# The second half of the delta heads: one exponential per head in a block behind the last query Silu, the norm factor by a GpSimd power

## The chip, the cores and the metric

The kernel runs on one core of a Trainium2 chip. The metric is the time of one execution on the device in microseconds. The kernel before has three timed runs, and one execution taken by the profiler.

## The reference, cut to what matters

One block of a network: modulated norm, projections, a dilated attention (8 heads) and a gated delta rule (8 heads) side by side, an output projection, and a feed-forward part. The change concerns the delta heads, 64 wide, over 1024 tokens.

```python
qkv = jax.nn.silu(_causal_conv(jnp.concatenate([q, k, v], axis=-1), conv_w))
...
q = _l2norm(q.reshape(shp)) * HEAD_DIM ** -0.5
k = _l2norm(k.reshape(shp))          # x * rsqrt(sum(x*x) + EPS)
...
gcum = jnp.cumsum(g...)              # per chunk
diff = gcum[..., :, None] - gcum[..., None, :]
decay = jnp.where(causal, jnp.exp(jnp.where(causal, diff, 0.0)), 0.0)
a_mat = jnp.where(strict, jnp.einsum('nbhcd,nbhed->nbhce', k_beta, kc) * decay, 0.0)
...
qk = jnp.where(causal, jnp.einsum('nbhcd,nbhed->nbhce', qc, kc) * decay, 0.0)
```

In the kernel a chunk has 128 tokens, so there are 8 chunks. For each head a tile of 128 keys x (8 chunks x 128 queries) holds `exp(G_query - G_key)` times the factor `rk` that normalises the key, and zero above the diagonal. Both score products are multiplied with it as they leave the accumulators.

## The kernel before

**Two halves of heads.** `delta(0)` handles heads 0 to 3, `delta(1)` heads 4 to 7. A half consists of: convolution and Silu of its keys and queries (`conv`, L550), their transposes and square sums (`delta_turn`, L729), the decay tiles and the score products (`delta_prep`, L754), the values (`delta_v`, L845), the inverse (`delta_inverse`, L867) and the scan over the chunks (`delta_scan`, L973). The convolutions, transposes and square sums of the second half's four tensors (cv0 and cv1 keys, cv2 and cv3 queries) are done in `delta_early` (L1195), which is called at the end of `delta(0)`. A finished one is stored to DRAM (L1202), and `delta(1)` loads it back (L1221).

**Fill.** TensorE (PE) does other projections between the steps of the delta part. `others()` (L1148) yields them in fixed order: z0, then kd, qd and vd of the second half, z1, then va, and key and query projections of the attention. Each of the first five is 20.48 us by its own count (8 tiles of 2.56 for z). `turn(name)` (L576) takes as much of it as the table `FILL` says for that step, and puts the step behind the last fill instruction on PE; `hold` (L1181) does the same ahead of an inverse, by `LEVELS`: 4 us behind qd for the first half, 46 us behind z1 for the second. The steps of the first half's inverse have 0.64 each, lc0_0 1.92; sb0_6 has 1.92, trq3_0False 2.56, kk1_0_0_q 6.4, kk1_0_0_k 0.64, trv2_0 12.8, trv3_0 10.24.

**What drains a z tile.** A tile of z is 24 matmuls (L613) into one of two accumulator banks with the tag "g"; `z_evac` (L630) drains it by a Silu on ScalarE (ACT, L634), GpSimd (POOL) multiplies it by the norm's gain (L635), and SyncE's queue (SP) stores it. All projections use these two "g" banks in turn.

**Order.** Each engine works through its instructions in the order in which the planner has put them; what is traced earlier has precedence, `urgent()` raises it, and `tc.issue_after(ins)` puts what is traced in its block behind `ins` on that engine. Buffers with one tag are used in turn: "dt" (two buffers) serves, one after the other, the first half's nt, tt and tn of the inverse, then cv0 to cv3, and then eb2 and eb3. "lu" (five) serves the decay tiles `dt0_*` and `dt1_*`, the values vd and the inverse U. "s" and "t" are two accumulator banks each.

**The decay tiles before.** `delta_rows` (L704) loads, for each head, the row of G broadcast to all partitions, and POOL cuts it at the diagonal with -1e30 (L716). `delta_prep` forms `lr = -0.5 * ln(rk + eps) - Gc` (L765, L766, L768) from the square sums `rk`, and `rk = exp(-0.5 * ln)` (L767). Then ACT does 32 exponentials of 128x128 for each half, one for every head and chunk, with `lr` as its bias (L771). Near its end `delta_prep` loads `eb` (rows of G for 64 partitions each, L832), takes its exponential (L839) and multiplies q by it on POOL (L840).

ACT holds one table of functions at a time; the profile shows a load (ACT_TABLE_LOAD) wherever Silu, Ln and Exp follow each other.

Of the kernel before, what the change touches and what calls it, by code (L numbers as in the profile page):

```python
# [10 lines left out]
F32 = mybir.dt.float32  # L11
F32R = mybir.dt.float32r
AF = mybir.ActivationFunctionType
# [5 lines left out]
P = 128  # L19
# [17 lines left out]
EPS = 1e-6  # L37
# [45 lines left out]
def build(tc, I, out):  # L83
# [35 lines left out]
    )  # L119
    eps1 = const([P, 1], "eps1")  # L120
    nc.vector.memset(eps1, EPS)
    mhalf = const([P, 4], "mhalf")
    nc.vector.memset(mhalf, -0.5)

    const([P, 88], "end")

    def small(name, shape, src):
        t = const(shape, name)
# [418 lines left out]
        wt = [scratch(f"wt{i}_", NF, [P, HALF]) for i in range(4)]  # L547


    def conv(ci, xp, dst):  # L550
        nc.scalar.activation(dst, xp, AF.Copy, scale=cw[:, ci, 3:4])
        for s_ in range(1, 4):
            nc.vector.scalar_tensor_tensor(
                out=dst[:, s_:T], in0=xp[:, 0 : T - s_], scalar=cw[:, ci, 3 - s_ : 4 - s_], in1=dst[:, s_:T],
                op0=ALU.mult, op1=ALU.add,
            )
        nc.scalar.activation(dst, dst, AF.Silu)

    kd, qd = {}, {}
    last, taken = [None], [None]  # L560
# [69 lines left out]
    def z_evac(g):  # L630
        def f(tb, ps):
            zt = pv.tile([P, 256], F32, name=f"zt{g}_{tb}", tag="ev", bufs=4)
            with urgent():
                taken[0] = nc.scalar.activation(zt, ps[:, 0:256], AF.Silu)  # L634
# [69 lines left out]
    def delta_rows(g):  # L704

        dts = []
        for hl_ in range(4):
            dt_ = pd.tile([P, 8, P], F32, name=f"dt{g}_{hl_}", tag="lu", bufs=5)
            nc.sync.dma_start(
                dt_,  # L710
                bass.AP(
                    tensor=_.G.tensor, offset=_.G[0:1, :].offset + (32 * g + hl_) * P,
                    ap=[[0, P], [4 * P, 8], [1, P]],
                ),
            )
            sel[g] = nc.gpsimd.affine_select(  # L716
                out=dt_, in_=dt_, pattern=[[0, 8], [1, P]], compare_op=ALU.is_ge, fill=-BIG,
                base=0, channel_multiplier=-1,
            )
            dts.append(dt_)  # L720
        return dts

    def delta_norms(g):
        n = {}
# [4 lines left out]
    def delta_turn(g, kind, q, src, norms=None, keep=False):  # L729

        hp = 2 * g + q
        if keep:
            ktt = pd.tile([P, 8, P], F32, name=f"kt{hp}", tag="kt", bufs=2)
        for hf in range(2):
            ps = sbank(f"tr{kind}{hp}_{hf}{norms is None}")
            with turn(f"tr{kind}{hp}_{hf}{norms is None}"):
              for j in range(4):
                nc.tensor.transpose(
                    ps[:, j * P : (j + 1) * P], src[:, (4 * hf + j) * P : (4 * hf + j + 1) * P], ident
                )  # L740
# [12 lines left out]

    def delta_prep(g, st, norms, kt, lts):  # L754

        rk, eq, nbp, nbg, kds, lr = (norms[k] for k in ("rk", "eq", "nbp", "nbg", "kds", "lr"))
        gs = slice(32 * g, 32 * g + 32)
# [1 line left out]
        def g3(t):  # L759
            return t[:, gs].rearrange("p (n h) -> p n h", n=8)  # L760

        eqf = eq.rearrange("p n h -> p (n h)")

        if g == 1:
            nc.scalar.activation(lr, rk, AF.Ln, bias=eps1)  # L765
        nc.vector.tensor_scalar(out=lr, in0=lr, scalar1=-0.5, scalar2=None, op0=ALU.mult)  # L766
        nc.scalar.activation(rk, lr, AF.Exp)  # L767
        nc.vector.tensor_tensor(out=lr, in0=lr, in1=g3(Gc), op=ALU.subtract)  # L768
        for h in range(4):
            for n in range(8):  # L770
                nc.scalar.activation(lts[h][:, n], lts[h][:, n], AF.Exp, bias=lr[:, n, h : h + 1])  # L771
# [50 lines left out]
        for q in range(2):  # L822
            hp = 2 * g + q
            with tc.issue_after(sel[g].ins):
                nc.gpsimd.tensor_tensor(
                    out=kt[q].rearrange("p n (e d) -> p n e d", e=2),
                    in0=kt[q].rearrange("p n (e d) -> p n e d", e=2),
                    in1=bc(kds[:, :, 2 * q : 2 * q + 2], 64), op=ALU.mult,
                )
            eb = pr.tile([P, 8, P], F32, name=f"eb{hp}", tag="dt", bufs=2)  # L830
            for e in range(2):
                nc.sync.dma_start(  # L832
                    eb[64 * e : 64 * e + 64],
                    bass.AP(
                        tensor=_.G.tensor, offset=_.G[0:1, :].offset + (32 * g + 2 * q + e) * P,
                        ap=[[0, 64], [4 * P, 8], [1, P]],
                    ),
                )
            nc.scalar.activation(eb, eb, AF.Exp)  # L839
# [350 lines left out]
    def fetch(i, name):  # L1190
        xp = pr.tile([P, T], F32, name=f"xp_{name}", tag="xp", bufs=2)
        nc.sync.dma_start(xp, _.pj[i])
        return xp

    def delta_early():  # L1195

        for j in range(4):
            kind, q = ("k", j) if j < 2 else ("q", j - 2)
            t = pr.tile([P, T], F32, name=f"cv{j}", tag="dt", bufs=2)
            conv((4 if kind == "k" else 0) + 2 + q, fetch(j, f"{kind}{2 + q}"), t)  # L1200
            delta_turn(1, kind, q, t, norms=norms[1])
            nc.sync.dma_start(_.cv[j], t)  # L1202

    marks = {}
    norms = [delta_norms(g) for g in range(2)]

    def delta(g):
        st = {}
        kt = []
        for j in range(4):  # L1210
# [9 lines left out]
            else:  # L1220
                nc.sync.dma_start(t, _.cv[j])  # L1221
                if kind == "k":
                    kt.append(delta_turn(g, kind, q, t, keep=True))
        delta_prep(g, st, norms[g], kt[0:2], delta_rows(g))
        if g == 1:
            until(lambda: "vd" in done)
        delta_v(g, st, [lambda q=q: vxp[q] if g == 0 else fetch(4 + q, f"v{2 + q}") for q in range(2)])
        delta_inverse(g, st)
        until(lambda: ("qd", "z1")[g] in done)
        delta_scan(g, st)  # L1230
        if g == 0:
            delta_early()

    delta(0)
    delta(1)
    until(lambda: EARLY - 1 in done)
    run(mods)

# [763 lines left out]
```

## Time and profile before

| | us |
|---|---|
| three runs | 1399.05, 1403.87, 1405.15 (median 1403.87) |
| the profiled execution | 1399.13 |
| its span | 1397.3 |
| mean granted clock of PE | 0.991 |
| PE busy | 1343.9 |
| VectorE (DVE) busy | 878.8 |
| ACT busy | 661.4 |
| POOL busy | 283.6 |

The span goes from the first instruction to the last on the engines. A row of a timeline gives the start, the duration, the engine, the line, and the tiles "out<-in"; brackets at its end show how long the engine sat idle before it, and what released it. A row of a group gives busy time and mean, then idle time and its releasers. PE's rows overlap by the depth of its pipeline, so the pitch between starts says more of its rate than a duration does. Matmul tiles carry names such as `g_z` (projection), `kk_q` and `kk_k` (score products), `trk`, `trq` and `trv` (transposes of keys, queries and values).

### The profile page before, as it was taken

The page shows a single profiled execution, that of the slowest core. Times are in us where ns is not written, and L with a number is a line of the kernel's source. Part 1 is how long each engine was busy: PE and PEld are TensorE (multiplying, and loading weights), DVE is VectorE, ACT ScalarE, POOL GpSimd, SP SyncE. Part 2 cuts the span into 40 slices and gives each one's busy share as a digit, 9 for nine tenths or more (in the row PEclk, how much of TensorE's full clock was granted, in tenths as well). Part 3 has the DMA queues.
Part 4 walks back from the last instruction along what each step waited for, and adds up shares of the span by engine and source line. Part 5 has one row for each costly group of instructions (what it writes and reads, how often), then busy time and mean ns, then how long its engine had stood idle before and what let it go on. Part 6 is the DMA issues. An engine that isn't in the chain of part 4 may idle for free.

```text
span 1397.3 us, 24428 instructions
## 1 busy us (share of the span) xinstructions
PE 1343.9 (96%) x8984; PEld 1109.9 (79%) x8984; DVE 878.8 (63%) x1677; ACT 661.4 (47%) x1287; POOL 283.6 (20%) x267
## 2 busy tenths in 40 slices
PE   8999999998999899999999999999999999999998
PEld 5778877888888777778877788888888888888876
DVE  3688484656836433676238977667575776474497
ACT  4498424356234254775157633333333333444455
POOL 2346412443213244443262000000000000000000
PEclk9999999999999999999999999999999999999999
DMA  8666575486352455541584355455453665766585
GB/s 310 230 190 168 160 212 168 131 259 184 106 152 69 124 141 177 152 110 58 187 269 151 113 159 181 158 163 173 133 200 108 213 210 191 255 222 192 195 262 197
DMA packets 169872, 245.68 MB, mean 176 GB/s; under 512 B 32566, under 2 KB 73831, under 8 KB 169752
## 3 DMA queue, kind: packets, MB, share of 16 engines
q1 hardware_dynamic: 169752, 244.12, 55.3%
q8 instruction: 71, 1.16, 0.3%
q14 instruction: 49, 0.40, 0.1%
HBM read 181.30 MB, written 67.48 MB: 178 GB/s over the span
## 4 chain that ended last, share of the span: by engine, by line
PE 53%; DVE 5%; DMA 3%; issue 2%; ACT 2%; POOL 1%; SPq 0%; DVEq 0%; ACTq 0%; POOLq 0%
PE wua L1596 9%; PE wga L1596 8%; PE X L1796 6%; PE wuc L1596 4%; PE wgc L1596 4%; PE wo L590 4%; PE g_a L590 3%; PE wgb L1596 2%; PE Z L1796 2%; PE Y L1796 2%; PE wub L1596 2%; PE y L1353 2%; PE tr L1332 2%; PE S L1308 1%; PE S L1309 1%
## 5 line engine op out<-in xcount | busy, mean ns | idle before, releaser
L1586 DVE TENSOR_TENSOR wl_db<-wr_db,wh_db 128x512 fp32r<-128x512 f32 x77 | 52.9, 690 | 66.4 <-ACT wh_db L1585 66.4
L1585 ACT CAST wh_db<-wr_db 128x512 fp32r<-128x512 f32 x77 | 47.4, 620 | 85.7 <-PE X L1796 39.4
L1312 DVE CUSTOM_DVE_ANT_0 X<-S,ng 128x512 f32<-128x512 f32 (+3 forms) x64 | 36.9, 587 | 57.2 <-PE S L1309 43.7
L1319 POOL TENSOR_SCALAR X<-X,sc 128x128 f32<-128x128 f32 (+7 forms) x64 | 48.7, 764 | 76.3 <-DVE sc L1318 72.3
L1796 PE MATMUL X<-wl_db,wh_da 128*128 128x512 f32 x160 | 62.4, 390 | 0.3 <-DVE wl_db L1586 0.3
L1796 PE MATMUL X<-wh_db,wl_da 128*128 128x512 f32 x160 | 62.3, 389 | 0.0
L1796 PE MATMUL X<-wh_db,wh_da 128*128 128x512 f32 x160 | 62.3, 389 | 0.0
L1317 ACT ACTIVATE X<-X,sc 128x128 f32<-128x128 f32 (+7 forms) x64 | 49.5, 775 | 24.3 <-DVE sc L1312 22.7
L1586 DVE TENSOR_TENSOR wl_da<-wr_da,wh_da 128x512 fp32r<-128x512 f32 x77 | 52.8, 685 | 3.7 <-ACT wh_da L1585 3.6
L1585 ACT CAST wh_da<-wr_da 128x512 fp32r<-128x512 f32 x77 | 47.5, 616 | 15.0 <-DMA wr_da<-ao_d 8.1
L590 PE MATMUL g_a<-hh,wh_a 128*128 128x512 f32 x128 | 52.7, 412 | 0.0
L590 PE MATMUL wo<-yl,wh_wo 128*128 128x512 f32 x128 | 50.6, 396 | 1.9 <-DVE yl L1416 1.9
L590 PE MATMUL g_a<-hh,wl_a 128*128 128x512 f32 x128 | 51.7, 404 | 0.0
L590 PE MATMUL wo<-yh,wh_wo 128*128 128x512 f32 x128 | 51.6, 406 | 0.0
L590 PE MATMUL g_a<-hl,wh_a 128*128 128x512 f32 x128 | 51.4, 401 | 0.0
L590 PE MATMUL wo<-yh,wl_wo 128*128 128x512 f32 x128 | 51.1, 399 | 0.0
L1332 PE MATMUL tr<-ident,X 128*128 128x128 f32 x288 | 45.8, 278 | 5.1 <-POOL X L1319 2.4
L1585 ACT CAST wh_wg_s<-wg_s 128x512 fp32r<-128x512 f32 x33 | 20.5, 623 | 57.6 <-PE wuc L1596 24.4
L1332 PEld LDWEIGHTS tr<-ident,X 128*128 128x128 f32 x288 | 32.8, 140 | 17.0 <-POOL X L1319 6.2
L231 POOL TENSOR_TENSOR wl_wo<-wr_wo,wh_wo 128x512 fp32r<-128x512 f32 x24 | 32.2, 1344 | 59.1 <-ACT wh_wo L230 54.9
L1585 ACT CAST wh_wu_s<-wu_s 128x512 fp32r<-128x512 f32 x33 | 20.4, 621 | 43.8 <-PE wga L1596 17.2
L1585 ACT CAST wh_wg<-wr_wg 128x512 fp32r<-128x512 f32 x31 | 19.2, 622 | 46.3 <-PE wua L1596 18.9
(553 smaller groups left out, 4370.0 us busy)
## 6 DMA issues: line engine op xcount, KB each, us to landing
wm<-in_wada SPq DMA_DIRECT2D x44, 512.0 KB, 6.3
wr_da<-ao_d SPq DMA_DIRECT2D x77, 256.0 KB, 3.1
wr_wu<-in_wu SPq DMA_DIRECT2D x50, 256.0 KB, 2.7
wr_wg<-in_wg SPq DMA_DIRECT2D x48, 256.0 KB, 2.9
ao_d<-a SPq DMA_DIRECT2D x44, 256.0 KB, 2.4
wr_wd<-in_wdn SPq DMA_DIRECT2D x44, 256.0 KB, 3.0
wr_db<-wt_d SPq DMA_DIRECT2D x44, 256.0 KB, 2.7
ao_d<-as SPq DMA_DIRECT2D x33, 256.0 KB, 2.0
```

The lines of the kernel that those rows point to most:

```text
L231: (eng or nc.gpsimd).tensor_tensor(out=lo[:, :n], in0=raw[:, :n], in1=hi[:, :n].bitcast(F32), op=ALU.subtract)
L590: last[0] = nc.tensor.matmul(ps, a[:, w0], b[k0 + k4][:, cs], start=(i == 0), stop=(i == n - 1))
L1308: nc.tensor.matmul(ps[:, 0 : c1 - c0], QS[:, qs], KS[:, c0:c1], start=True, stop=False)
L1312: nc.vector.tensor_tensor_reduce(out=X[:, c0:c1], in0=ps[:, 0 : c1 - c0], in1=ng[:, u + c0 : u + c1], scale=1.0, scalar=(3e38 if m is None ...
L1317: nc.scalar.activation(X[:, 0:nk], X[:, 0:nk], AF.Exp, scale=-1.0, bias=m, accum_out=sc[:, 2:3])
L1319: nc.gpsimd.tensor_scalar(out=X[:, 0:nk], in0=X[:, 0:nk], scalar1=sc[:, 3:4], scalar2=0.0, op0=ALU.mult, op1=ALU.add)
L1332: nc.tensor.transpose(ps[:, (kb - c0) * P : (kb - c0 + 1) * P], X[:, kb * P : kb * P + P], ident)
L1353: ins = nc.tensor.matmul(yps[64 * e : 64 * e + 64, (q % 4) * P : (q % 4 + 1) * P], va[:, kb, 64 * e : 64 * e + 64], ets[q % 2][e][:, kb, : ...
L1585: nc.scalar.copy(hi, src)
L1586: (eng or nc.vector).tensor_tensor(out=lo, in0=src, in1=hi.bitcast(F32), op=ALU.subtract)
L1596: nc.tensor.matmul(ps, a[:, w0], b, start=(first and k == 0 and n_ == 0), stop=(k == 3 and n_ == 2), skip_group_check=True,)
L1796: nc.tensor.matmul(bank[b], a[:, ts_], w, start=(first and n_ == 0), stop=(last and n_ == 2), skip_group_check=True,)
```

## The change

The first half is computed as before. For the second half:

- `delta_early` stores cv ahead of its transposes, and behind the Silu of the last query (cv3) it calls the new `delta_exps`: the four decay rows are loaded and cut, DVE subtracts Gc from each, ACT takes one exponential of 128x1024 for each head, and then those of eb2 and eb3; the six stand in this order behind the Silu.
- Every Silu that is traced after that, those of `conv` and of `z_evac`, is put behind the last of the six (`behind`).
- `rk` is formed by POOL at the end of each key's turn: `(rk + EPS) ** -0.5`, on 16 elements of each partition. `delta_prep` has no Ln and no Exp of the norm in this half; DVE multiplies each decay tile by `rk` instead, 128x1024 each.
- `mhalf` grows from 4 to 16 columns, and a pad of the constants shrinks by 12.

```diff
-    mhalf = const([P, 4], "mhalf")
+    mhalf = const([P, 16], "mhalf")
...
-    const([P, 88], "end")
+    const([P, 76], "end")
...
+    behind = [None]
+
     def conv(ci, xp, dst):
...
-        nc.scalar.activation(dst, dst, AF.Silu)
+        with tc.issue_after(behind[0].ins) if behind[0] else ExitStack():
+            return nc.scalar.activation(dst, dst, AF.Silu)
...
     def z_evac(g):
...
-            with urgent():
+            with urgent(), tc.issue_after(behind[0].ins) if behind[0] else ExitStack():
                 taken[0] = nc.scalar.activation(zt, ps[:, 0:256], AF.Silu)
...
(delta_rows)
+            if g:
+                nc.vector.tensor_tensor(
+                    out=dt_, in0=dt_, op=ALU.subtract,
+                    in1=bc(Gc[:, 32 * g : 32 * g + 32].rearrange("p (n h) -> p n h", n=8)[:, :, hl_], P),
+                )
             dts.append(dt_)
         return dts
+
+    def delta_exps(last):
+
+        lts = delta_rows(1)
+        ebs = [delta_eb(1, q) for q in range(2)]
+        for t in (*lts, *ebs):
+            with tc.issue_after(last.ins):
+                last = nc.scalar.activation(t, t, AF.Exp)
+        behind[0] = last
+        return lts, ebs
+
+    def delta_eb(g, q):
+
+        eb = pr.tile([P, 8, P], F32, name=f"eb{2 * g + q}", tag="dt", bufs=2)
+        for e in range(2):
+            nc.sync.dma_start(
+                eb[64 * e : 64 * e + 64],
+                bass.AP(
+                    tensor=_.G.tensor, offset=_.G[0:1, :].offset + (32 * g + 2 * q + e) * P,
+                    ap=[[0, 64], [4 * P, 8], [1, P]],
+                ),
+            )
+        return eb
...
(delta_turn)
+        if norms and kind == "k" and g:
+            v = norms["rk"][:, :, 2 * q : 2 * q + 2]
+            nc.gpsimd.tensor_scalar(out=v, in0=v, scalar1=EPS, scalar2=None, op0=ALU.add)
+            nc.gpsimd.tensor_tensor(
+                out=v, in0=v, in1=mhalf.rearrange("p (n e) -> p n e", e=2), op=ALU.pow,
+            )
...
-    def delta_prep(g, st, norms, kt, lts):
+    def delta_prep(g, st, norms, kt, lts, ebs):
...
-        if g == 1:
-            nc.scalar.activation(lr, rk, AF.Ln, bias=eps1)
-        nc.vector.tensor_scalar(out=lr, in0=lr, scalar1=-0.5, scalar2=None, op0=ALU.mult)
-        nc.scalar.activation(rk, lr, AF.Exp)
-        nc.vector.tensor_tensor(out=lr, in0=lr, in1=g3(Gc), op=ALU.subtract)
-        for h in range(4):
-            for n in range(8):
-                nc.scalar.activation(lts[h][:, n], lts[h][:, n], AF.Exp, bias=lr[:, n, h : h + 1])
+        if g == 0:
+            nc.vector.tensor_scalar(out=lr, in0=lr, scalar1=-0.5, scalar2=None, op0=ALU.mult)
+            nc.scalar.activation(rk, lr, AF.Exp)
+            nc.vector.tensor_tensor(out=lr, in0=lr, in1=g3(Gc), op=ALU.subtract)
+            for h in range(4):
+                for n in range(8):
+                    nc.scalar.activation(lts[h][:, n], lts[h][:, n], AF.Exp, bias=lr[:, n, h : h + 1])
+        else:
+            for h in range(4):
+                nc.vector.tensor_tensor(out=lts[h], in0=lts[h], in1=bc(rk[:, :, h], P), op=ALU.mult)
...
-            eb = pr.tile([P, 8, P], F32, name=f"eb{hp}", tag="dt", bufs=2)
...
-            nc.scalar.activation(eb, eb, AF.Exp)
+            if ebs:
+                eb = ebs[q]
+            else:
+                eb = delta_eb(g, q)
+                nc.scalar.activation(eb, eb, AF.Exp)
...
(delta_early, for each of the four)
-            conv((4 if kind == "k" else 0) + 2 + q, fetch(j, f"{kind}{2 + q}"), t)
+            last = conv((4 if kind == "k" else 0) + 2 + q, fetch(j, f"{kind}{2 + q}"), t)
+            nc.sync.dma_start(_.cv[j], t)
+            if j == 3:
+                made = delta_exps(last)
             delta_turn(1, kind, q, t, norms=norms[1])
-            nc.sync.dma_start(_.cv[j], t)
+        return made
...
-        delta_prep(g, st, norms[g], kt[0:2], delta_rows(g))
+        delta_prep(g, st, norms[g], kt[0:2], *(made or (delta_rows(g), None)))
...
-        if g == 0:
-            delta_early()
+        return None if g else delta_early()
...
-    delta(0)
-    delta(1)
+    delta(1, delta(0))
```

More of the change, by code (lines that the diff above doesn't have):

```diff
@@ L829, in delta_prep @@
                 )
-            eb = pr.tile([P, 8, P], F32, name=f"eb{hp}", tag="dt", bufs=2)
[L831 to L839, printed above, removed]
+            if ebs:
[3 more added lines that the diff above has]
+                nc.scalar.activation(eb, eb, AF.Exp)
             nc.gpsimd.tensor_tensor(
@@ L1199, in delta_early, with delta @@
             t = pr.tile([P, T], F32, name=f"cv{j}", tag="dt", bufs=2)
-            conv((4 if kind == "k" else 0) + 2 + q, fetch(j, f"{kind}{2 + q}"), t)
+            last = conv((4 if kind == "k" else 0) + 2 + q, fetch(j, f"{kind}{2 + q}"), t)
+            nc.sync.dma_start(_.cv[j], t)
+            if j == 3:
+                made = delta_exps(last)
             delta_turn(1, kind, q, t, norms=norms[1])
-            nc.sync.dma_start(_.cv[j], t)
+        return made
     marks = {}
     norms = [delta_norms(g) for g in range(2)]
-    def delta(g):
+    def delta(g, made=None):
         st = {}
```

## The prediction

> **What bounds the kernel now.** I read the page's engine shares first, then the busy time by stretch around the change, then who waits for whom on PE there, then the timelines.
>
> ```profile
> PE 1343.9 (96%) x8984; PEld 1109.9 (79%) x8984; DVE 878.8 (63%) x1677; ACT 661.4 (47%) x1287; POOL 283.6 (20%) x267
> 305.00:315.00 10.00, 9.14 (x98) 8.19 (x96) 4.50 (x13) 9.81 (x16) 4.07 (x5) 1.00 0.92 320
> 315.00:325.00 10.00, 10.00 (x91) 8.91 (x90) 4.76 (x9) 9.48 (x27) 6.82 (x5) 1.00 0.75 245
> 335.00:345.00 10.00, 6.24 (x63) 5.70 (x63) 5.63 (x8) 3.56 (x4) 0.64 (x2) 0.77 0.62 167
> 345.00:355.00 10.00, 10.00 (x100) 9.67 (x99) 6.24 (x6) 1.91 (x4) 0.95 (x1) 0.89 0.34 98
> ```
>
> PE is busy 96% of the span, so over the whole kernel an idle microsecond of PE is a microsecond of time, unless something later waits anyway. In the stretches the columns are length, then busy time of PE, PEld, DVE, ACT and POOL, then the clock. From 305 to 325 us ACT is full too (9.81 and 9.48 of 10). But PE keeps running beside it (9.14 and 10.00); it loses time only behind it, at 335:345 (6.24), where the clock falls to 0.77 and is still 0.89 in the next stretch.
>
> ```profile
> PE trv L857 <- ACT vd L557: 3.8, 1, 3.8
> PE yt L1065 <- DVE o L1055: 1.2, 1, 1.2
> PE trq_0False L738 <- ACT cv L557: 0.9, 1, 0.9
> PE kk_q L800 <- DMA qd<-cv_d: 0.9, 1, 0.9
> PE kk_k L800 <- DVE qk L806: 0.3, 1, 0.3
> ```
>
> Those are all of PE's waits from 285 to 345 us: 7.1 us in sum. Only the first is long: the first value transpose of the second half (trv2, L857) waits for a Silu that ACT gives late. Everything else of ACT's load is covered by projections that fill PE (z1 at L613, then va). That cover is the point on which the change turns:
>
> ```profile
> 260.99 0.37 PE L613 MATMUL g_z<-wh_z,hh 128*128 128x256 f32 x1
> ...
> 278.59 0.38 ACT L634 ACTIVATE zt<-g_z 128x256 f32<-128x256 f32 x1 [0.33 <-PE g_z L613]
> 286.98 0.38 ACT L634 ACTIVATE zt<-g_z 128x256 f32<-128x256 f32 x1 [1.35 <-PE g_z L613]
> 289.86 0.38 ACT L634 ACTIVATE zt<-g_z 128x256 f32<-128x256 f32 x1 [2.50 <-DMA zl<-zg_d]
> ...
> 313.88 0.37 ACT L634 ACTIVATE zt<-g_z 128x256 f32<-128x256 f32 x1
> ```
>
> The rows of ACT are drains of the z1 projection: eight tiles of 24 matmuls in two "g" banks. The first tile starts at 260.99, tile 0 is drained at 278.59, tile 1 at 286.98, tile 2 at 289.86, tile 7 at 313.88.
>
> **The change, part by part.**
>
> *ACT gets lighter.*
>
> ```profile
> L771 ACT ACTIVATE dt<-dt,lr 128x128 f32<-128x128 f32 x32 | 9.7, 397 | 0.0
> L765 ACT ACTIVATE lr<-rk,eps 128x32 f32<-128x32 f32 x1 | 0.3, 321 | 0.0
> L767 ACT ACTIVATE rk<-lr 128x32 f32<-128x32 f32 x1 | 0.2, 229 | 0.0
> 303.12 1.28 ACT L765 ACT_TABLE_LOAD   x1
> L839 ACT ACTIVATE eb<-eb x4: 1039/1045/1058, 143.2 to 330.0; 128x1024 f32<-128x1024 f32 x4
> ```
>
> Removed for the second half: 32 small exponentials (9.7 us), Ln and Exp of the norm (0.3 and 0.2). Added: 4 of 128x1024 as L839's, 1.05 each, 4.2. The two of eb move. Six table loads in this part (before L765, twice back to Silu, L767, L771, and L557 of vd) become two, 4 x 1.28 = 5.1 saved. ACT loses 9.7 + 0.5 + 5.1 - 4.2 = 11.1 us. On the path only what PE waited for counts: the 3.76 us at trv2 and the 0.27 at kk_k can go, 4.0 in sum.
>
> *DVE and POOL get heavier.*
>
> ```profile
> L875 DVE TENSOR_TENSOR nt<-nt,bpr x2: 1216/1221/1226, 172.1 to 353.2; 128x1024 f32<-128x1024 f32 x2
> L1053 POOL TENSOR_TENSOR of<-of,mhalf x16: 1006/1007/1122, 252.6 to 472.3; 128x4 f32<-128x4 f32 x16
> 302.53 2.59 DVE L553 SCALAR_TENSOR_TENSOR cv<-xp_q,cw,cv 128x1022 f32<-128x1022 f32 x2
> ```
>
> Four subtractions of Gc and four multiplications by rk, each 128x1024 with a broadcast operand as L875: 8 x 1.22 = 9.8 us of DVE. The subtractions stand around the two query convolutions, whose last step (L553) ends at 302.53 + 2.59 = 305.1. One row tile is loaded long before, so three can get in the way: between 0 and 3 x 1.22 = 3.7 us later; I take 0, because the convolution is traced ahead of them. The multiplications hide behind z1 matmuls that PE still has to do (below); without that cover they would cost 4.9. On POOL two adds and two powers on 16 elements for Ln and Exp: a power of 4 elements takes 1.01, so 16 lie between 1.01 and 4 x 1.01; POOL is busy 4.07 of 10 us at 305:315, and rk is first used after that. Zero. The larger mhalf is paid for by the smaller pad: no address moves.
>
> *What is moved, and the wait it makes.* The block (4 row loads, 4 selects on POOL, 4 subtractions, 4 + 2 exponentials, 4 half loads of eb) goes from the second half's preparation to behind the Silu of cv3. And every Silu traced later must stand behind the block on ACT. The fill that the program takes ahead of its steps can be added up: until qd is done 62.1 us, 4.5 by LEVELS, 11.5 at the sixteen steps of the four inverses, 1.9 at sb0_6, together 80.0 when the block is traced; z1 begins at 4 x 20.48 = 81.92. So all eight drains of z1 come behind it, those that ran at 278.59 and 286.98 too. Queued behind them: tile 2 of z1 needs tile 0's bank, and the rest of z1, va and kk1_0_0 (which waits for 6.4 us of fill, into tile 2) come after it. PE runs out when tile 1 is done, at about 286.9, and stays so until the block ends.
>
> When does it end? Its last link is the exponential of eb3. That tile takes the buffer of cv3 ("dt", two buffers), so it waits until cv3 is transposed and its store has landed.
>
> ```profile
> 306.54 1.06 ACT L557 ACTIVATE cv<-cv 128x1024 f32<-128x1024 f32 x1
> ...
> cv_d<-cv SPq DMA_DIRECT2D x3, 512.0 KB, 6.3
> eb<-G_d SPq DMA_DIRECT2D x4, 256.0 KB, 5.1
> dt<-G_d SPq DMA_DIRECT2D x4, 512.0 KB, 7.4
> ```
>
> DVE done at 305.1; the Silu, without the Ln and Silu loads ahead of it, ends at 306.3 (now 306.54 + 1.06). Store issued 306.4, landed after 6.3: 312.7. Two half loads of eb3, the second issued 0.6 later, landed after 5.1: 318.4. SP is in order, and if the loads of eb2, which wait for cv2's store, stand ahead of cv3's store, that adds some 3. The exponential 1.05, the load of the Silu table 1.28, the drain of tile 0 at 0.38 and some 0.9 for semaphores and for issue: PE goes on at about **322**. With everything late (DVE 3.7, SP 3) it is 329; with a DMA system less loaded because PE stands, say both landings 1.5 shorter, 319.
>
> What did PE do between 286.9 and 322 before?
>
> ```profile
> L613 PE MATMUL g_z<-wl_z,hh 128*128 128x256 f32 x49 | 14.2, 289 | 0.0
> L613 PE MATMUL g_z<-wh_z,hh 128*128 128x256 f32 x48 | 13.9, 290 | 0.0
> L613 PE MATMUL g_z<-wh_z,hl 128*128 128x256 f32 x48 | 13.6, 284 | 0.0
> L800 PE MATMUL kk_q<-qd,kd 64*128 64x128 f32 x32 | 3.0, 293 | 0.9 <-DMA qd<-cv_d 0.9
> L613 PE MATMUL g_va<-wh_va,hh 128*128 128x256 f32 x6 | 1.9, 318 | 0.0
> ```
>
> 49 + 48 + 48 = 145 matmuls of z1, 3 x 6 = 18 of va; one starts every 0.12 us (drains at 286.98 and 289.86, 24 matmuls apart). They are shut out: 145 x 0.12 = 17.4, and 18 x 0.12 = 2.2. The transposes, yt and the modulation matmuls stay possible. Of the score products (L800) 32 ran in that time. Now the half that lies in "t" banks (64 of 128) isn't held by the fill and can run once cv3 is loaded back, the other half can't. Between 0 and 64 at about 0.1 us (3.0 us busy for 32 that overlap in part): from +3.2 to -3.2. I take the same 32, so 0.
>
> *Clock.*
>
> ```profile
> 341.73 1.97 PE L857 MATMUL trv<-ident,vd 128*128 128x128 f32 x8 [3.76 <-ACT vd L557]
> ...
> 351.41 1.03 PE L857 MATMUL trv<-ident,vd 128*128 128x128 f32 x8
> ```
>
> After the wait of 3.76 eight transposes take 1.97 us, where the next eight take 1.03, and the clock is below full for about 5.5 us (0.89 over ten means 2.2 at half the clock after 345, behind 3.3 from 341.73 on); at the full pitch they would need half as long, so some 2.4 us were lost. The page "TensorE: Matmul & The Clock Gate" of the Trainium skill (The HAM clock gate) says that the array falls to half its clock after an idle window of about 3.4 us and needs as long a busy one to come back; the trace agrees on the half rate, with 5.5 us for its return. By that rule, too, a long hole costs the same single return as a short one. So the hole pays 2.4 once on its far side, and the stall that it removes no longer does: 0.
>
> *Does a later wait swallow it?* After the values PE must do 46 us of fill before the second half's inverse goes on:
>
> ```profile
> 393.08 1.78 DVE L923 STREAM_TRANSPOSE U<-tn 32x256 f32<-32x256 f32 x4 [7.04 <-DMA tn<-tn_d]
> 406.54 1.75 DVE L930 TENSOR_TENSOR cs<-lv,nbp 32x256 f32<-32x256 f32 x4 [11.68 <-PE lv L918]
> ```
>
> DVE had the inverted blocks at 393.08, and then waited 11.68 us for PE. So the chain by DVE has more than 10 us of slack, PE leads, and PE's lag goes through undiminished.
>
> **Sum:** 17.4 + 2.2 + 0 - 4.0 + 0 = **+15.6 us**. The profiled execution takes 1399.13 (span 1397.3): 1414.7. The three runs are 1399.05, 1403.87 and 1405.15; the mean of the four is 1401.8, and on that base I say **1417**. With 322 replaced by 319 or 329 (-3, +7) and the score products at their ends (-3.2, +3.2), the likeliest case lies between +9.4 and +25.8: 1411 to 1428.
>
> **Rivals.**
>
> *A, the turns move up (the other side).* With PE empty, the transposes of cv0 could run before the last flips, and everything behind them earlier.
>
> ```profile
> L557 ACT ACTIVATE cv<-cv x3: 1056/1057/1059, 244.3 to 306.5; 128x1024 f32<-128x1024 f32 x3
> 280.65 0.55 PE L999 MATMUL st<-R,U 128*128 128x64 f32 x4
> ...
> 292.31 0.60 PE L738 MATMUL trk_0False<-ident,cv 128*128 128x128 f32 x4
> ```
>
> For it: two Silus of cv were done by 245 (first at 244.3), but the first turn ran at 292.31. Against it: it ran right behind the last flip although z1, traced later, had been running since 261; the "s" banks seem to be given in order of the program. The row loads need the buffers of the first half's U, last read at 280.65 + 0.55, and land after 7.4 us; then come select, subtraction, six exponentials, a table load and a drain, some 11 us, so the block ends at 300 at best. From 322 that is -22: 15.6 - 22 = -6.4, so 1395. It decides at 306, where the sum is zero. Chance 0.10.
>
> *B, the change doesn't hold the drains of z1* (the order isn't binding, or the block runs early enough). Then ACT's 11.1 us are free: trv2's and kk_k's waits (4.0), the clock's return (2.4) and the waits at trq and kk_q (1.8) go: -8.2, 1394. For it: ACT at 9.81 and 9.48. The page "ScalarE: Activation LUTs" of the Trainium skill (Rules for kernel authors) advises to do all of one table set before switching, which this change does; by its figure of about 2.7 us for a switch (an estimate; the rows here show 1.28 for the load itself) ACT would save 10.8 instead of 5.1, still beside a PE that waited 4.0. Against it: the order is written on every Silu traced later. Chance 0.08.
>
> *C, the hole is larger than its matmuls.* If copies and squares that serve the turns of kd are queued behind eb3 on ACT, the first half of the score products comes only after 329, with DVE's 4.9 us of multiplying uncovered ahead of it, and the values wait for ACT as they do now (the 4.0 stay): 15.6 + 7 + 4.0 = +26.6, 1428. Chance 0.15.
>
> *D, absorbed.* The second half's scan leaves PE gaps that the late fill takes over, or half of the hole is closed: about +5, 1407. Against it: a fill that is late is also late for the attention that needs it. Chance 0.12.
>
> The forecast keeps 0.55. Less than 0.5% (7 us) can't be told from no change here. Faster: B's 0.08 and 0.04 of A's, 0.12. Same: the other 0.06 of A, 0.07 of D, 0.01 at the forecast's edge, 0.14. Slower: 0.74. The range from 1402 to 1430 leaves out A and B.
>
> **What would show it.** Right: PE idle from about 287 with waits on the drain of z1 (L634), the first drain of z1 at 320 to 325 instead of 278.59, behind an eb exponential that waits for a DMA; two table loads in place of six; no wait at trv2; the same 11 us of DVE wait for PE before the inverse. Wrong: z1 drains before 300, or the lag of PE gone before the inverse.

## The result, and the profile after

| | us |
|---|---|
| before, four runs beside it | median 1403.9 (1399.05 to 1405.15) |
| the change, four runs | median 1435.32 (1434.35 to 1439.76) |
| ratio | 1.0236, 95% interval 1.0204 to 1.0269 |
| the profiled execution of the change | 1439.76, span 1438.0, mean granted clock of PE 0.973 |

The change makes the kernel slower by 2.0 to 2.7%, which is 29 to 38 us. The forecast was slower by 15.6 us, to 1417, in a range from 1402 to 1430: the sign is right, but the size is about half of what was measured, and the measured time lies above the range. Where nothing else is said the lines below are of the changed kernel, in which the code stands 3 to 35 lines further down (L634 is now L637, L738 is L769, L1018 is L1052).

Busy time by stretch around the change; the columns are those of the prediction's windows:

```profile
250.00:260.00 10.00, 6.23 (x32) 5.75 (x32) 5.03 (x12) 0.90 (x3) 4.91 (x4) 0.76 0.63 226
255.00:265.00 10.00, 9.43 (x39) 8.98 (x40) 4.84 (x19) 0.91 (x3) 2.07 (x3) 0.51 0.28 90
300.00:310.00 10.00, 6.45 (x112) 3.50 (x104) 1.12 (x5) 0.53 (x2) 0.00 (x0) 0.65 0.93 334
310.00:320.00 10.00, 6.10 (x50) 4.32 (x50) 4.63 (x7) 4.50 (x7) 3.53 (x3) 0.67 0.76 244
320.00:330.00 10.00, 2.03 (x9) 1.64 (x9) 10.00 (x14) 4.07 (x6) 7.86 (x4) 0.50 0.35 119
330.00:340.00 10.00, 6.15 (x32) 4.76 (x33) 9.85 (x12) 8.56 (x10) 0.00 (x0) 0.50 0.76 246
350.00:360.00 10.00, 9.66 (x98) 8.54 (x99) 6.47 (x11) 0.38 (x1) 5.06 (x3) 0.96 0.16 34
```

PE was nearly full from 305 to 335 us before. Now there is a hole from 295 to 345 (PE works 2.03 of the ten microseconds from 320 on, at half the clock), and a second, smaller one at 250:260 that no step of the prediction has; behind it the clock stays at half (0.51 over 255:265). The hole's end, in ACT's timeline:

```profile
329.81 1.06 ACT L560 ACTIVATE cv<-cv 128x1024 f32<-128x1024 f32 x1 [1.97 <-DVE cv L555]
330.88 1.28 ACT L737 ACT_TABLE_LOAD   x1
332.18 3.90 ACT L737 ACTIVATE dt<-dt 128x1024 f32<-128x1024 f32 x4
335.98 1.04 ACT L737 ACTIVATE eb<-eb 128x1024 f32<-128x1024 f32 x1
...
341.84 1.06 ACT L737 ACTIVATE eb<-eb 128x1024 f32<-128x1024 f32 x1
342.92 1.28 ACT L637 ACT_TABLE_LOAD   x1
344.21 0.66 ACT L637 ACTIVATE zt<-g_z 128x256 f32<-128x256 f32 x2
```

This is the predicted block: the Silu of cv3, one table load, the four exponentials of dt, those of eb (eb3's comes 4.8 us after the end of eb2's, with other copies and short waits between them), the load of the Silu table, and only then the drains of tiles 0 and 1 of z1. The first drain comes at 344.21, not at 322. What precedes it shows why. On SP, first before the change and then in it, and then on DVE, again before and in the change, and on PE:

```profile
283.84 1.90 SPq L1120 DMA_DIRECT2D wm<-in_wada  x2
285.84 0.42 SPq L1045 DMA_DIRECT2D zl<-zg_d  x1
```

```profile
288.51 1.06 SPq L1079 DMA_DIRECT2D zl<-zg_d  x1
...
293.03 14.13 SPq L1154 DMA_DIRECT2D wm<-in_wada  x10
307.21 0.46 SPq L1079 DMA_DIRECT2D zl<-zg_d  x1
```

```profile
291.49 0.43 DVE L1055 TENSOR_TENSOR o<-o,zl 128x256 f32<-128x256 f32 x1 [5.27 <-DMA zl<-zg_d]
```

```profile
312.70 0.43 DVE L1089 TENSOR_TENSOR o<-o,zl 128x256 f32<-128x256 f32 x1 [5.10 <-DMA zl<-zg_d]
```

```profile
313.82 1.06 PE L769 MATMUL trk_0False<-ident,cv 128*128 128x128 f32 x4
```

Ten loads of the modulation weights (wm) stand on SP ahead of the load of zl for the first half's last flip, where there were two. That flip waits for zl until 312.70 (291.49 before), and the transposes of cv0, which stand behind it on PE, begin at 313.82 instead of 292.31. From there to the first drain it is 30.4 us; the prediction had 29.7 (292.3 to 322). So the block is as long as forecast and begins 21.5 us late.

A part of that lateness arises earlier. DVE (before, then in the change) and PE in the first half's scan:

```profile
248.53 0.94 DVE L1018 COPY S<-st 64x64 f32<-64x64 f32 x4 [4.33 <-PE st L1009]
```

```profile
252.68 2.27 DVE L724 TENSOR_TENSOR dt<-dt,Gc 128x1024 f32<-128x1024 f32 x1 [6.23 <-POOL dt L719]
254.96 0.95 DVE L1052 COPY S<-st 64x64 f32<-64x64 f32 x4
```

```profile
255.57 0.76 PE L1019 MATMUL st<-S,kd 128*128 128x128 f32 x2 [3.77 <-DVE S L1052]
```

The first subtraction of Gc stands on DVE ahead of the scan's first state copy. It waits 6.23 us for POOL, which waits 3.46 us for the row's load, and the copy with everything behind it on DVE waits too. (The subtraction itself took 2.27 us, the other three 1.21 to 1.23.) The copy begins at 254.96, where it was 248.53. Of these 6.4 us 2.2 were there before the subtraction: the multiplications of the first half's inverse that read cs (lv) begin at 219.6 in this execution, at 217.3 in that of before. PE stands for 3.77 us, and then runs at half its clock until about 265.5. The last zl load but one is issued at 288.51, where it was 279.32. So of the 21.5 us 2.2 were there already, some 7.0 come from the early subtraction (the delay of the copy, and the half clock behind it), and some 12.2 from the ten loads (21.4 us at the last zl, 307.21 against 285.84, less the 9.2 at the one before).

What PE waited for between 245 and 500 us, the four largest (total, times, longest):

```profile
PE mods L211 <- DMA wm<-in_wada: 6.4, 9, 1.4
PE trq_0False L769 <- ACT cv L560: 5.7, 2, 5.1
PE ps_bp L820 <- DVE nbp L814: 4.8, 1, 4.8
PE st L1019 <- DVE S L1052: 3.8, 1, 3.8
```

Inside a hole the waits are named after whatever ran next; no row names the drain of z1 (L637) as the cause, since PE always had a small step of the other chain in between. The hole is read from the windows and from ACT, not from this list. The row of trv (3.8 before) is gone from it. And the row that decides whether the lag lasts:

```profile
444.39 1.75 DVE L964 TENSOR_TENSOR cs<-lv,nbp 32x256 f32<-32x256 f32 x4 [23.68 <-PE lv L952]
```

DVE waits 23.68 us for PE ahead of the second half's inverse (11.68 before), and goes on 37.85 us later than before (444.39 against 406.54). From here to the span's end both executions take about the same: 993.6 and 990.8 us. The beginning of this row is therefore a good place in a trace to read off what a version costs; over the profiled executions below the rest is 989 to 997 us. It also carries what an execution had lost before the stage of the change, and this differs: the first half's lv begins at 217.34 before, and between 217.55 and 221.67 in the versions. One execution each doesn't show whether that belongs to the version, so versions are compared below by the loss less this part.

### The profile page after: what moved, and what is told of

It is laid out like the page before. It is cut to its first block, busy times and chain, and to the rows that moved or that the text cites. A ratio compares the mean times of both kernels' runs of the same rounds, so it can differ in the third digit from the quotient of the medians.

```text
span 1438.0 us, 24391 instructions
## 1 busy us (share of the span) xinstructions
PE 1361.6 (95%) x8984; PEld 1122.0 (78%) x8984; DVE 885.7 (62%) x1683; ACT 651.3 (45%) x1253; POOL 289.5 (20%) x271
## 4 chain that ended last, share of the span: by engine, by line
PE 53%; DVE 5%; DMA 3%; issue 2%; ACT 2%; POOL 0%; DVEq 0%; SPq 0%; ACTq 0%; POOLq 0%
PE wua L1631 8%; PE wga L1631 8%; PE X L1831 6%; PE wo L593 5%; PE wgc L1631 4%; PE wuc L1631 4%; PE g_a L593 3%; PE Z L1831 3%; PE y L1388 2%; PE wgb L1631 2%; PE Y L1831 2%; PE wub L1631 2%; PE tr L1367 2%; PE S L1343 1%; DVE X L1347 1%
## 5 line engine op out<-in xcount | busy, mean ns | idle before, releaser
L1620 ACT CAST wh_da<-wr_da 128x512 fp32r<-128x512 f32 x77 | 47.5, 616 | 15.7 <-DMA wr_da<-ao_d 9.6
```

The costliest lines, as they stand in the source:

```text
L1620: nc.scalar.copy(hi, src)
```

## The experiments

Ratios are to the kernel before on the same chip; its medians in the groups of runs were 1399.7 to 1403.9, so ratios are compared, not times. "Loss at lv" is the beginning of DVE's row above, less 406.54, from one profiled execution each; "there already" is the beginning of the first half's lv, less 217.34.

| version | median | ratio (95%) | first drain of z1 | loss at lv | there already |
|---|---|---|---|---|---|
| the change | 1435.32 | 1.0236 (1.0204 to 1.0269) | 344.21 | 37.9 | 2.2 |
| drains free | 1410.86 | 1.0070 (1.0045 to 1.0095) | 285.38 | 10.4 | 0.2 |
| late subtractions | 1431.91 | 1.0229 (1.0195 to 1.0263) | 341.48 | 34.1 | 3.4 |
| late modulation loads | 1426.35 | 1.0168 (1.0129 to 1.0207) | 333.33 | 28.3 | 4.3 |
| both of these | 1416.83 | 1.0125 (1.0097 to 1.0152) | 324.63 | 18.2 | 3.6 |
| both, hold ends at dt | 1417.92 | 1.0108 (1.0080 to 1.0136) | 314.25 | 14.4 | 1.9 |
| before, with the hold alone | 1424.25 | 1.0157 (1.0128 to 1.0187) | 326.71 | 26.0 | 2.8 |
| free and late | 1406.48 | 1.0035 (1.0018 to 1.0053) | 279.91 | 4.4 | 1.3 |
| unheld, eb late | 1404.93 | 1.0024 (1.0003 to 1.0044) | 281.06 | 7.1 | 0.3 |
| the same, nbp's transpose late | 1402.84 | 1.0015 (1.0002 to 1.0028) | 281.87 | 4.5 | 1.2 |
| free and late, nbp's transpose late | 1406.40 | 1.0052 (1.0036 to 1.0069) | 280.71 | 4.7 | 2.0 |
| unheld, nbp behind the convolution too | 1407.34 | 1.0039 (1.0016 to 1.0062) | 281.54 | 6.9 | 2.7 |
| unheld, the values' copy late too | 1406.69 | 1.0042 (1.0023 to 1.0062) | 280.55 | 5.2 | 2.1 |

**1. The drains of z1 free.** The Silus of `z_evac` are no longer put behind the block; all else is the change.

```diff
-            with urgent(), tc.issue_after(behind[0].ins) if behind[0] else ExitStack():
+            with urgent():
                 taken[0] = nc.scalar.activation(zt, ps[:, 0:256], AF.Silu)
```

> The changed kernel, but the Silus that drain z1 are no longer put behind the block of six exponentials (those of the value convolutions still are). Theory 'starvation': the loss comes from PE having nothing to do while z1's drains are held; z1 drains again near 279 us and the modulation loads go back behind the last load of zl; what is left is the first subtraction of Gc that stands in VectorE's queue ahead of the scan of the first half (about 7 us), less what the lighter ScalarE saves (up to 6): 1404 to 1411, middle 1407. Rival 'new work': the eight passes of 128x1024 on VectorE, the powers on GpSimd and the longer chain cost the time themselves: 1428 or more.

Measured 1.0070: the hold, with what it draws after it, carries some 23 of the 33 us that 2.36% are. The modulation loads are back in pairs between those of zl, without being touched. The early subtraction is still there: st waits 3.7 us for the state copy, and the first drain comes 6.8 us later than before the change (285.38 against 278.59), 0.2 of which were there already. And a new wait of the same order has come: PE waits 7.7 us at the transposes of cv3, because ACT has another instruction ahead of that Silu, which waits for its load:

```profile
319.85 1.15 ACT L553 ACTIVATE vd<-xp_v,cw 128x1024 f32<-128x1024 f32 x1 [7.72 <-DMA xp_v<-pj_d]
320.90 1.04 ACT L560 ACTIVATE cv<-cv 128x1024 f32<-128x1024 f32 x1
```

**2 to 4. The two order effects, one by one and together.** Late subtractions: they stand behind the last step of the last query convolution on DVE (`step` is that step). Late modulation loads: those traced after the block lose their urgency.

```diff
+                with tc.issue_after(step[0].ins):
                     nc.vector.tensor_tensor(out=dt_, in0=dt_, op=ALU.subtract, ...)
...
-                with urgent(), tc.issue_after(...):
+                with ExitStack() if behind[0] else urgent(), tc.issue_after(...):
```

> The changed kernel, but the four subtractions of Gc on VectorE stand behind the last step of cv3's convolution, so that none is in the queue ahead of the first half's scan. Theory: the state copy of the scan at 254.96 moves back to about 250.8, PE's wait of 3.77 us and the half clock behind it go, 7 us in all: 1428 (1425 to 1431). Rival 'absorbed': the scan only runs earlier into the same hole, which ends by another chain: 1433 to 1437.

> The changed kernel, but the modulation loads traced after the block are no longer urgent. Theory: they were moved ahead of the load of zl for the last flip (307.21 instead of 285.84), and the transposes of cv0 (313.82) waited for that flip; without it these run 12 us earlier, the drains of z1 begin near 332 instead of 344, and some modulation matmuls that ran in the hole come later (4 us): 1423 to 1429, middle 1426. Rival 'harmless filler': the modulation only used a hole that lasts until the exponentials anyway: 1433 to 1438.

> The changed kernel with both: subtractions behind cv3's convolution and modulation loads not urgent; the hold on z1's drains stays. Theory: only the hole of the forecast is left, from about 287 to 322 us: 1417 (1412 to 1422). If the two add up to nothing and the hole has another floor: 1428 to 1436.

Late subtractions alone bring nothing that the ratio can tell (1.0229 against 1.0236; the intervals are too wide for 5 us). At lv, less what was there already, they bring 5.0 us (35.62 to 30.65), where 7 were expected: the scan is 1.7 us late here too, at the last zl load but one, behind a short fall of the clock at 258:262 (0.69 and 0.50). The ten loads are still drawn ahead of the last zl (288.96 to 303.59). Late modulation loads alone bring 11.7 us at lv, and 9.5 by the ratio. Both together bring 21.0 us at lv, to 1.0125, with the load of the last zl back at 287.84. That is more than the sum of the two (16.6), and late subtractions bring 9.3 us where the modulation loads are late as well; whether the two act on each other, one execution of each doesn't show. With both gone, the block stands where the prediction had put it, from the transposes of cv0 at 294.83 on:

```profile
308.25 1.06 ACT L561 ACTIVATE cv<-cv 128x1024 f32<-128x1024 f32 x1 [0.53 <-DVE cv L556]
...
322.26 1.06 ACT L739 ACTIVATE eb<-eb 128x1024 f32<-128x1024 f32 x1 [0.57 <-DMA eb<-G_d]
323.33 1.28 ACT L638 ACT_TABLE_LOAD   x1
324.63 0.66 ACT L638 ACTIVATE zt<-g_z 128x256 f32<-128x256 f32 x2
```

First drain at 324.63 (forecast 322, up to 329; 3.6 us were there already), 29.8 us after the first transpose of cv0 (forecast 29.7). The time is 1.0125 (the forecast, 15.6 on 1401.8, is 1.011), 17.5 us by the ratio and 14.7 at lv less what was there. So the forecast had one mechanism rightly sized, and two others were missing.

**5. The hold ends at dt's last exponential** instead of eb3's, on the version with both edits.

```diff
                 last = nc.scalar.activation(t, t, AF.Exp)
-        behind[0] = last
+                if t is lts[3]:
+                    behind[0] = last
```

> The version with late subtractions and late modulation loads, but the hold ends at the last of the four exponentials of dt, not at eb3's. Theory (the hole lasts as long as the hold, and its last 7 us are the wait for eb3's load): first drain of z1 at about 317 instead of 324.6, tiles 2 and 3 run while eb2 and eb3 come, some 5 us of z1 more in the hole: 1411, between 1408 and 1414. Rival (the end of the hold is not what sets the time; what comes after it, the scores and values, waits anyway): 1415 to 1419, as the version it is made from.

```profile
314.25 0.66 ACT L638 ACTIVATE zt<-g_z 128x256 f32<-128x256 f32 x2
314.93 1.28 ACT L739 ACT_TABLE_LOAD   x1
...
327.40 0.38 ACT L638 ACTIVATE zt<-g_z 128x256 f32<-128x256 f32 x1 [1.67 <-PE g_z L617]
337.67 0.38 ACT L638 ACTIVATE zt<-g_z 128x256 f32<-128x256 f32 x1 [9.88 <-PE g_z L617]
```

The drains start 10.4 us earlier (1.6 of them there already), but tiles 2 and 3 then leave PE only at 327.40 and 337.67, 4.9 and 5.2 us earlier than in the version it is made from: PE is at half its clock until about 321, and takes transposes and score products in between, those from 327.29 to 334.50 at the full clock. At lv 2.2 us of the expected 5 arrive, less what was there already; the ratio (1.0108) can't be told from that of the version it is made from (1.0125), and the time lies in the rival's range. As to the mechanism, an earlier end of the hold is worth less than its length says.

**6. The hold alone, on the kernel before.** No exponential is moved and no arithmetic changed: the drains of z1 that are traced behind the Silu of cv3 stand behind it.

```diff
-            with urgent():
+            with urgent(), tc.issue_after(behind[0].ins) if behind[0] else ExitStack():
                 taken[0] = nc.scalar.activation(zt, ps[:, 0:256], AF.Silu)
...
+            if j == 3:
+                behind[0] = last
```

> The kernel before with one edit: z1's drains traced behind the Silu of cv3 must stand behind it on ACT. No exponential, no arithmetic of the change. Theory (the hold by itself starves PE, and the empty fill by itself draws the modulation loads ahead of the last zl): ten loads of wm ahead of zl of the last flip, that flip at about 310 instead of 291.5, first drain of z1 at about 328 instead of 278.6, PE waits there, 1420, between 1412 and 1428. Rival (the loss needs the block: its exponentials, the wait for eb3, the early subtraction): 1402 to 1409.

```profile
288.13 15.19 SPq L1122 DMA_DIRECT2D wm<-in_wada  x10
303.37 0.46 SPq L1047 DMA_DIRECT2D zl<-zg_d  x1
```

1.0157, 22 us, without a block, without a wait for eb3, without a subtraction. The same ten loads stand ahead of the same zl. So it is the hold of the drains by itself that draws them forward, and experiment 3 shows that it does so by their urgency. The likely reason, which no run shows by itself: with z1 shut out, the modulation matmuls are the next work that PE can do at that place, and their loads come with them. And a hold that ends with a Silu, not after six exponentials, is enough, with the loads that it draws, to lose two thirds of the whole.

**7 and 8. What is left of the change without hold and early subtraction.** Free and late combines the edits of 1 and 2. In the unheld one no Silu is held, and the exponentials of eb stay where they were before the change:

```diff
-        ebs = [delta_eb(1, q) for q in range(2)]
-        for t in (*lts, *ebs):
+        for t in lts:
             with tc.issue_after(last.ins):
                 last = nc.scalar.activation(t, t, AF.Exp)
-        behind[0] = last
-        return lts, ebs
+        return lts, None
```

> The change without both of its order effects: z1's drains are not held behind the block, and the subtractions of Gc stand behind the last step of the last query convolution. Theory (what is left of the change when the hold and the early subtraction are gone is a wash: ACT has 11 us less to do, DVE 10 us more, both beside a busy PE): 1404, between 1399 and 1408, with z1's first drain at about 280, the first state copy of the first half's scan at about 249 as before, and no idle stretch of PE over 4 us between 250 and 345. Rival (the early subtraction is worth nothing, as its removal alone seemed to show): the time of the run with the drains free, 1409 to 1412.

> The arithmetic of the change alone: one exponential per head, behind the Silu of cv3, the norm by POOL's power, late subtractions; no Silu is held, and the exponentials of eb stay where they were before the change. Theory (the hold is what costs, the arithmetic is a wash): 1403, between 1397 and 1408, within 0.5% of the kernel before. Rival 1 (the values' Silu, which waits in the change behind the whole block, was worth keeping held, since the table stays loaded): slower than the run with the block kept, by 3 or more. Rival 2 (DVE's 9.8 us are what costs): 1411 or more, with waits of PE on the multiplied rows (L8xx, kk_k).

1.0035 and 1.0024: nearly a wash, as expected, though both intervals lie above 1. Free and late is faster than drains free with the early subtraction still in it (1.0070), so here that subtraction costs some 5 us by the ratio and 7.0 at lv; the rival is out. But the expectation of no idle stretch over 4 us failed. In the run free and late, the power on POOL, nbp on DVE, and its transpose on PE:

```profile
299.50 3.77 POOL L788 TENSOR_TENSOR rk<-rk,mhalf 128x16 f32<-128x16 f32 x1
...
305.76 2.94 POOL L788 TENSOR_TENSOR rk<-rk,mhalf 128x16 f32<-128x16 f32 x1
```

```profile
308.73 0.19 DVE L816 SCALAR_TENSOR_TENSOR nbp<-beta,rk 128x32 f32<-128x32 f32 x1 [4.67 <-POOL rk L788]
```

```profile
308.98 0.39 PE L822 MATMUL ps_bp<-ident,nbp 128*32 128x128 f32 x1 [4.46 <-DVE nbp L816]
```

A power of 16 elements takes 2.94 and 3.77 us, near the upper bound of the prediction (1.01 to 4.04), and PE waits for its consequence, in a place where the trace of before had z1 running.

**9 to 12. Can the rest be had, so that the change gains?** First the transpose of nbp was put behind those of kd on PE, with and without the values held; then, on the unheld version, nbp and kds behind the convolution on DVE; then the copies that begin the values' convolution behind the exponentials on ACT.

```diff
+        with tc.issue_after(turned[0].ins):
             nc.tensor.transpose(ps[:32, 0:P], nbp.rearrange("p n h -> p (n h)"), ident)
...
+        with tc.issue_after(step[0].ins):
             nc.vector.scalar_tensor_tensor(out=nbp, ...)
...
+        with tc.issue_after(done_[0].ins) if done_[0] else ExitStack():
             nc.scalar.activation(dst, xp, AF.Copy, scale=cw[:, ci, 3:4])
```

> The run with the exponentials unheld, and one edit more: the transpose of nbp on PE (ps_bp) stands behind the last transposes of kd instead of ahead of the second half of z1. Theory (what is left of the change's cost there is PE standing 4.5 us at ps_bp, because the power on POOL took 3.8 and 2.9 us and nbp waits for it, plus about 2.4 us of the clock's return): 1398, between 1393 and 1402, a ratio to the kernel before of about 0.997, with no wait at ps_bp and clock 1.00 at 310:320. Rival (the wait is only passed on, to the scores or to the values): 1403 to 1408, as without the edit.

> The same edit on the run with free drains and late subtractions, where the Silus of the values and the exponentials of eb stay in the block: theory 1399, between 1394 and 1403; rival 1404 to 1408.

> The run with the exponentials unheld and the transpose of nbp late, and one edit more: on DVE nbp, nbg and kds, which wait for POOL's power, stand behind the last step of the last query convolution instead of ahead of it. Theory (the 4.7 us that PE waited at the transposes of cv3 came from DVE standing 4.69 us at nbp for POOL, with the convolution queued behind it): no wait at trq over 1 us, the Silu of cv3 at about 307 instead of 312, clock 1.00 at 310:320: 1397, between 1392 and 1401, a ratio to the kernel before of 0.994 to 0.999. Rival (the wait moves on again, or ACT's alternating table loads hold the rest): 1402 to 1406, ratio 1.001 or more.

> The run before this one (unheld, late transpose of nbp, nbp behind the convolution) with one edit more: the copies that begin the values' convolution stand on ACT behind the exponentials of dt. Theory (ACT stood 6.3 us for the load of xp_v ahead of the exponentials and of two drains of z1, and PE stood 5.1 us for those drains): no wait of PE over 3 us between 285 and 345, clock 1.00 from 290 to 340: 1398, between 1393 and 1402, ratio 0.994 to 1.001. Rival (the wait goes on to the values' own transposes, trv, or the gain is eaten by two more table loads on ACT): 1403 to 1408.

In all four the wait went on, as the rivals said; the times (1402.84, 1406.40, 1407.34 and 1406.69) lie in the rivals' ranges or within 1.4 us of them. Each edit removed the wait that it was aimed at, and one of about the same length appeared at the next link. In the first two PE waits 4.7 us at the transposes of cv3, since nbp also stands on DVE ahead of that convolution:

```profile
310.62 0.19 DVE L815 SCALAR_TENSOR_TENSOR nbp<-beta,rk 128x32 f32<-128x32 f32 x1 [4.69 <-POOL rk L787]
```

With nbp behind the convolution the Silu of cv3 is at 307.61, but ACT then stands for the load of xp_v ahead of the drains of z1's last tiles, and PE for those:

```profile
315.68 1.15 ACT L555 ACTIVATE vd<-xp_v,cw 128x1024 f32<-128x1024 f32 x1 [6.26 <-DMA xp_v<-pj_d]
```

```profile
320.95 0.58 PE L618 MATMUL g_va<-wh_va,hh 128*128 128x256 f32 x1 [5.08 <-ACT zt L639]
```

With that copy late, PE waits at the next transposes:

```profile
327.47 0.95 PE L773 MATMUL trk_0True<-ident,kd 128*128 128x128 f32 x4 [4.96 <-ACT sqq L779]
```

1.0015 to 1.0052: each interval lies above 1, so a small loss stays; no version tried was faster than the kernel before. What sets the length of that last wait isn't settled by these runs.

## Why the prediction was half right

**PE is the bound, and an idle microsecond there is one of time.** Right as far as PE's lag ahead of the second inverse goes: the loss at lv (with or without what was there already) and the ratio, taken of 1400 us, agree in every row of the table within 5 us.

**All eight drains of z1 are held.** Right. None ran before 344.21, and freeing them gave back 23 of 33 us.

**The block's length.** Right: 30.4 us from the first transpose of cv0 to the first drain, forecast 29.7, with eb3's exponential as its last link and two table loads in place of six. Some of that agreement is luck: up to the end of cv3's Silu it took 17.1 us (forecast 14.0), and from there on 13.3 (forecast 15.7). With both order effects gone the parts are right too: 14.5 and 15.3. And 32 score products ran ahead of z1's next matmul, as many as the prediction took.

**The block's beginning: the step that failed.** The prediction took the trk turn at 292.31 as fixed (its 322 is counted from 305.1 and 306.3, times of the kernel before) and asked only what stands behind the block. Two instructions came in ahead of it. The subtractions were put at 0 "because the convolution is traced ahead of them"; that compares them with the convolution alone, while the neighbour in DVE's queue was the scan's state copy; instead of 0, the first one made the scan some 7.0 us late. And the modulation bursts, which the prediction left in their places ("the modulation matmuls stay possible"), moved ahead of the last zl on SP, which made it another 12.2 us late. Both together are worth 15.5 us by the ratios (2.36% against 1.25%) and 21.0 at lv; the forecast hole itself was 17.5 us by its ratio against 15.6 predicted.

**The gain of 4.0 at trv2 and kk_k.** The wait at trv2 did go, and ACT's busy time fell by 10.1 us (661.4 to 651.3; forecast 11.1). In the change its going says little of the lighter ACT, since the z1 matmuls left over from the hole keep PE busy at that place. Without the hole the 4.0 were not to be had: in all seven versions with free drains a wait of 4.5 to 7.7 us stands at another link of the same chain. There the term should have been about 0: the prediction didn't ask what is late next where a stall goes.

**The multiplications and POOL's power at zero.** In the change this holds: nbp runs at 329.69 without a wait, behind DVE's other work. Without the hole the power does cost, through nbp; "rk is first used after that" overlooked that nbp uses it and that PE's transpose of nbp stands in order ahead of z1.

**The clock: one return of 2.4 us.** Behind the hole it is about right. In the changed kernel the z1 matmuls start every 0.21 us from 347.44 to 350.60 and every 0.12 after it, which loses some 1.4 us, and the score products since 345.44 ran at half the clock too, some 1.0. The Trainium skill, "TensorE: Matmul & The Clock Gate" (What's actually happening), asks for about 3.4 us of sustained work until the clock returns; here PE had been at work nearly without a gap since 345.44, so the trace shows 5.2 us, longer than the page says, as the 5.5 before the change were. But there were two falls, not one. After the stall of 3.77 us at the state copy the clock stayed at half until about 265.5, 9.9 us after PE had begun again at 255.57, although PE was at work all that time; why so long, no run shows. The prediction has no term for that fall, as it has no stall there. Its 2.4 itself is a little low: half of its 5.5 us is 2.75.

**No later wait swallows the lag.** Right, and more so: DVE's wait for PE grew from 11.68 to 23.68 us. It doesn't measure PE's lag alone (the prediction expected the same 11 us), because DVE's own part came less late (it had the inverted blocks at 418.92, 25.8 us later than before) than PE's fill.

**The rivals.** C was nearest in size (1428), by another mechanism. A had the sign of the turns' move wrong: they moved back by 21.5 us. B's price for free drains, a gain of 8.2, was wrong too: with the drains free the versions still lose 0.15 to 0.7%. D didn't come: nothing later took up the lag.

## What to carry to other kernels

Work that fills the bottleneck engine must be able to leave it: before a long operation is grouped on another engine, count which drains of accumulators stand behind it, for a hold of the drains alone, with the loads that it drew forward, cost 1.6% here. When a hold takes a whole stream of fill away, ask what the planner will put in its place, and in which queue that lands (here ten urgent loads on SP ahead of one small load on the chain). And price a removed wait at nothing until the next link of its chain has been looked at: three edits in a row each moved a wait of some five microseconds one link on.

## What was not expected of the hardware

POOL's power with a tensor exponent took 2.92 to 3.98 us for 16 elements of each partition over the versions, where the one of 4 elements took 1.01: its time grew with the elements of a partition, at most nearly fourfold. Why the same 16 elements took 2.9 us in one place and nearly 4 in another, no run shows. The kernel of experiment 6 loads the table twice for Ln and Exp with no Silu in between (1.28 us each, at 319.76 and 321.88, with only a square of sqq after the Ln), so as loaded there the two functions came from different sets.
